# Two hybrid encoder layers on eight cores: a rewrite with subtiles, scheduled engines, packed weights and layer norm per subtile

## The chip, the cores and the metric

The kernel runs on the eight cores of one Trainium2 chip. Each core works alone on half of one sequence (2048 tokens, with 256 more in front as halo), in two passes of up to 1152 tokens. The metric is the device time of the slowest core in microseconds. The record sorts the executions into fast and slow ones. The first kernel's slow runs took 3552.8 and 3639.2 us, its fast ones 3271.4 and 3274.5. Only fast runs are compared. A ratio below is the record's: the fast runs of one kernel over the first kernel's fast runs of the same rounds. It is not quite the ratio of quoted medians. Short names: PE is the matmul engine (TensorE), PEld its weight loads, DVE is VectorE, ACT ScalarE, POOL GpSimd.

## The reference, cut to what matters

```python
for l in range(2):
    ada = (silu(c) @ w_ada[l] + b_ada[l])[:, None, :]          # conditioning, 6 x 1024 per sequence
    sh1, sc1, gt1, sh2, sc2, gt2 = split(ada, 6)
    h = x * (1 + sc1) + sh1
    z = h @ w_in[l] + b_in[l]                                  # 1024 -> 9216
    zb, zc, zx, zu, zv, zp, zg = split(z)
    y_a = (zb * conv3(zc * zx)) @ w_a_out[l]                   # branch A
    y_b = spatial_gating(gelu(zu), gelu(zv), ...) @ w_b_out[l] # branch B, norm of v, 128 x 128 blocks
    y_c = multiscale_pool(zp, w_pool[l], pool_scale[l])        # branch C
    g_a, g_b, g_c = split(sigmoid(zg), 3)
    x = layer_norm(ALPHA * x + gt1 * ((g_a*y_a + g_b*y_b + g_c*y_c) @ w_o[l]))
    h = x * (1 + sc2) + sh2
    up_a, up_g = split(h @ w_up[l] + b_up[l], 2)               # 1024 -> 2 x 2816
    f = gelu(conv3(up_a) + b) * up_g
    x = layer_norm(ALPHA * x + gt2 * (f @ w_down[l]))
```

## The kernel before

Data lie feature-major on chip: 128 features on the partitions, tokens along the free axis. One projection of all tokens of a pass fills three PSUM banks (PA or PB), and one VectorE or ScalarE instruction works on all of them.

```python
def fm_proj(lhs_list, rhs_fn, geo, P=None):
    off, nseg, seglen = geo                    # e.g. 3 pieces of 386 tokens
    if P is None:
        P = big_ps()                           # PA and PB in turn
    for j in range(nseg):
        for k in range(nk):
            mm(P[:, j, 0:seglen], lhs_list[k], rhs_fn(k, ...), k == 0, k == nk - 1, ...)
    return P[:, 0:nseg, 0:seglen]
```

Weights lie in memory as the reference has them; a load of 128 columns takes runs of 512 bytes. There are four slots of 4096 columns. All engines run in the order in which the program was written. The layer norm of a stage starts when the sums over all its tokens are there:

```python
def layer_norm_fm(c0, T, outs):                # T up to 1152
    ... S1, S2 = ones-matmuls over all tokens
    ts(mean, S1, 1.0 / D, ALU.mult)
    ... stt(rstd, S2, 1.0 / D, rstd, ALU.mult, ALU.subtract)
    act_op(rstd, rstd, AF.Sqrt, bias=epsc[:, 0:1])
    reciprocal(rstd)
    for c in range(8):
        tt(yh, r, meanf, ALU.subtract); tt(yh, yh, rstdf, ALU.mult)
        for dst_fn, sc_fn, b_fn in outs:       # back to xT, and the next h
            act_op(dst_fn(c), yh, AF.Identity, bias=b_fn(c), scale=sc_fn(c))
```

The input comes token-major and is transposed by TensorE (128 x 128 fp32), as is the output. The conditioning weights (24 loads of 1024 x 512) are worked off between other steps by a `tick()`.

## Time and profile before

| | |
|---|---|
| fast runs | 3271.4 and 3274.5 us |
| slow runs | 3552.8 and 3639.2 us |
| cores in the profiled run | 3261 to 3290 us, mean clock 0.913 to 0.922 |
| PE, DVE, ACT busy | 80, 47, 30% |

How to read it: PE is the busiest engine and the chain that ended last passes through it for 59% of the span, yet a fifth of the span it stands. The prediction shows the lines and cuts a layer into stages. Two more groups matter for what the change removes. They are from the view of instruction groups by shape; after the bar stand the busy time in us, the mean in ns, and the idle time of the engine just before with what ended it.

```profile
L324 ACT ACT_TABLE_LOAD x87 | 111.6, 1283 | 235.1 <-DVE tmp L328 86.8 <-DVE tmp L341 68.9 <-PE PA L304 35.2
...
L455 DVE RECIPROCAL tmp<-tmp 128x1152 f32<-128x1152 f32 x4 | 29.4, 7352 | 10.9 <-ACT tmp L324 10.9
```

A reciprocal of 1152 columns holds VectorE for 7.35 us while PE has nothing to do, and 87 activation table loads cost ScalarE 112 us.

### The profile page before, as it was taken

The numbers are of one execution on the slowest core, as the hardware profiler recorded it, in microseconds if no ns is written. First come the engines' busy times: TensorE is split into PE (matmuls) and PEld (weight loads), VectorE is DVE, ScalarE is ACT, GpSimd is POOL, SyncE is SP. The second block draws the span as 40 slices with busy tenths as digits, with TensorE's granted clock in tenths as the row PEclk, the third lists the DMA queues.
The fourth block names the chain that finished last, engine by engine and source line by source line (L and its number), as shares of the span: only waits on it lengthen the run. The fifth ranks groups of instructions, "written<-read, shape, count | busy, mean of one in ns | idle before, by whom it ended". The sixth has DMA issues, their size and how long they took to land.

```text
span 3290.1 us, 41682 instructions; the slowest of 8 cores (3261.2 to 3290.1 us)
## 1 busy us (share of the span) xinstructions
PE 2635.8 (80%) x17020; PEld 1594.4 (48%) x17020; DVE 1532.3 (47%) x1518; ACT 980.3 (30%) x905; POOL 285.0 (9%) x324
## 2 busy tenths in 40 slices
PE   3887798589598795888499699499959969949994
PEld 2553455356365563664355355255525535525552
DVE  3322435654643437454442433745364243374535
ACT  1112312443223313441222412444232241244412
POOL 1210000010110000101010000000101000001000
PEclk9998999799899997999699899799979989969997
DMA  9996736244564345447364232434536423234441
GB/s 172 122 131 93 109 58 92 39 65 54 56 77 66 52 71 64 53 65 83 122 70 72 39 54 50 64 52 56 63 29 77 65 39 58 39 51 58 52 53 58
DMA packets 348316, 225.39 MB, mean 69 GB/s; under 512 B 104416, under 2 KB 342112, under 8 KB 347616
## 3 DMA queue, kind: packets, MB, share of 16 engines
q0 software_dynamic: 341504, 198.20, 46.2%
q1 hardware_dynamic: 6624, 24.53, 2.2%
q8 instruction: 137, 2.24, 0.3%
q14 instruction: 51, 0.42, 0.0%
HBM read 412.50 MB, written 8.39 MB: 128 GB/s over the span
## 4 chain that ended last, share of the span: by engine, by line
PE 59%; DVE 18%; ACT 12%; DMA 5%; issue 4%; DVEq 0%; ACTq 0%; POOL 0%; SPq 0%; POOLq 0%
PE PA L304 31%; PE PB L304 23%; ACT tmp L324 7%; DVE tmp L341 5%; DVE tmp L328 3%; PE PC L304 2%; PE PD L304 2%; ACT L324 2%; DVE ubuf L328 2%; DMA wsl<-w_in 2%; DVE big L341 2%; DVE tmp L455 2%; DMA tmp<-xs 2%; ACT ubuf L324 1%; ACT hT L324 1%
## 5 line engine op out<-in xcount | busy, mean ns | idle before, releaser
L304 PE MATMUL PA<-hT,wsl 128*128 128x386 bf16 (+2 forms) x6336 | 1033.2, 320 | 295.4 <-DVE hT L345 217.2
L304 PEld LDWEIGHTS PA<-hT,wsl 128*128 128x128 bf16 x6336 | 618.5, 99 | 674.1 <-issue 333.0
L304 PE MATMUL PB<-hT,wsl 128*128 128x386 bf16 (+2 forms) x3264 | 521.8, 316 | 69.2 <-DVE big L341 49.7
L304 PEld LDWEIGHTS PB<-hT,wsl 128*128 128x128 bf16 x3264 | 312.6, 98 | 265.6 <-issue 97.4
L324 ACT ACTIVATE tmp<-PA,vecs_s 128x1158 f32<-128x1158 f32 (+2 forms) x200 | 229.8, 1149 | 685.7 <-PE PA L304 684.4
L341 DVE SCALAR_TENSOR_TENSOR tmp<-tmp,vecs_s 128x1156 f32<-128x1156 f32 (+2 forms) x240 | 318.1, 1325 | 238.4 <-ACT tmp L324 225.9
L324 ACT ACTIVATE tmp<-tmp,vecs_s 128x1158 f32<-128x1158 f32 (+2 forms) x208 | 246.1, 1183 | 420.3 <-DVE tmp L341 321.8
L304 PE MATMUL PB<-preT,wsl 128*128 128x386 bf16 (+2 forms) x1728 | 275.7, 313 | 4.1 <-DMA wsl<-w_a_out 3.5
L304 PE MATMUL PA<-big,wsl 128*128 128x384 bf16 (+2 forms) x1320 | 231.1, 333 | 8.3 <-DVE big L328 5.9
L277 POOL DMA_DIRECT2D wsl<-w_in x144 | 126.2, 886 | 1257.0 <-PE PA L304 548.3
L304 PE MATMUL PB<-big,wsl 128*128 128x384 bf16 (+2 forms) x1320 | 228.3, 331 | 0.0
L304 PEld LDWEIGHTS PB<-preT,wsl 128*128 128x128 bf16 x1728 | 166.6, 97 | 98.3 <-issue 5.5
L324 ACT ACTIVATE tmp<-xT 128x1152 f32<-128x1152 f32 (+2 forms) x72 | 77.4, 1085 | 387.4 <-DVE xT L341 387.4
L304 PE MATMUL PC<-wsl,hT 128*128 128x512 bf16 x560 | 142.6, 401 | 53.2 <-DVE tmp L328 48.9
L324 ACT ACT_TABLE_LOAD x87 | 111.6, 1283 | 235.1 <-DVE tmp L328 86.8
L304 PEld LDWEIGHTS PA<-big,wsl 128*128 128x128 bf16 x1320 | 130.5, 99 | 101.5 <-issue 11.1
L341 DVE SCALAR_TENSOR_TENSOR big<-PB,vecs_s,tmp 128x1158 bf16<-128x1158 f32 (+2 forms) x88 | 116.7, 1326 | 133.0 <-ACT tmp L324 114.6
L304 PEld LDWEIGHTS PB<-big,wsl 128*128 128x128 bf16 x1320 | 130.3, 99 | 90.0
L304 PE MATMUL PD<-wsl,hT 128*128 128x512 bf16 x560 | 143.8, 403 | 23.9 <-DVE tmp L328 16.0
L341 DVE SCALAR_TENSOR_TENSOR tmp<-PB,vecs_s,tmp 128x1158 f32<-128x1158 f32 (+2 forms) x48 | 63.6, 1326 | 186.5 <-PE PB L304 94.3
L277 POOL DMA_DIRECT2D wsl<-w_up x88 | 77.0, 883 | 690.3 <-PE PB L304 690.3
L328 DVE TENSOR_TENSOR big<-PB,tmp 128x1158 f32<-128x1158 f32 (+2 forms) x32 | 40.6, 1267 | 200.3 <-PE PB L304 160.7
(117 smaller groups left out, 1840.3 us busy)
## 6 DMA issues: line engine op xcount, KB each, us to landing
wsl<-w_in POOLq DMA_DIRECT2D x48, 1024.0 KB, 9.6
wsl<-w_up POOLq DMA_DIRECT2D x88, 512.0 KB, 7.8
wsl<-w_ada POOLq DMA_DIRECT2D x24, 1024.0 KB, 19.8
wsl<-w_in POOLq DMA_DIRECT2D x96, 256.0 KB, 6.2
wsl<-w_down POOLq DMA_DIRECT2D x32, 704.0 KB, 7.1
tmp<-xs SPq DMA_DIRECT2D x18, 512.0 KB, 4.7
wsl<-w_a_out POOLq DMA_DIRECT2D x8, 1024.0 KB, 8.2
wsl<-w_b_out POOLq DMA_DIRECT2D x8, 1024.0 KB, 12.1
```

The source lines that it names most:

```text
L277: items.append((lambda e, dst=dst, src=src: e.dma_start(out=dst, in_=src), (), (dst,)))
L304: R.op("pe", lambda e: e.matmul(o, l, r, start=start, stop=stop), reads=(l, r), writes=(o,), signal=signal)
L324: R.op("act", lambda e: e.activation(out=out, in_=in_, func=func, bias=bias, scale=scale), reads=rd, writes=(out,))
L328: R.op(eng, lambda e: e.tensor_tensor(out=out, in0=in0, in1=in1, op=op), reads=(in0, in1), writes=(out,))
L341: R.op(eng, lambda e: e.scalar_tensor_tensor(out=out, in0=in0, scalar=scalar, in1=in1, op0=op0, op1=op1), reads=rd, writes=(out,))
L455: R.op("dve", lambda e: e.reciprocal(out=rstd, in_=rstd), reads=(rstd,), writes=(rstd,))
```

## The change

The intent: PE should never stand. Nearly every instruction works on a subtile of at most 388 columns (512 in the v and z blocks), so that each projection takes one of eight PSUM banks, and a pass over the recorded program picks, engine by engine, what can start first. x and y are feature-major in memory, weights are packed so that each load reads one contiguous run per partition, the three gated branches are merged in one stage (with tanh in place of sigmoid, meant to spare table loads), and each subtile has its own layer norm, in which ScalarE's ln and exp take the place of the square root and the reciprocal. Cut to the core:

```diff
-class Rec:                       # engines in program order
+class Prog:
+    def schedule(self):          # list scheduling with a cost for each operation
+        while left:
+            for e in ENGS:
+                for op in avail[e]:
+                    est = op.ready if op.ready > f else f
+                    key = (est, op.prio)
+                    ...          # earliest start first, then program order
+            if op.dma:
+                t0 = max(est + cost + 1300.0, dma_free)
+                dma_free = t0 + op.nbytes / 320.0
...
-NSLOT = 4
-SLOT_ELEMS = 4096
+NW = 14                          # weight area: 14 units of 1024 columns
+UNIT = 1024
+class Units:                     # picks the free run of units that was given back longest ago
...
-        w_in = din("w_in", [DEPTH, D, DIN])
+        wmixa_d = din("wmixa", [DEPTH, 8, 128, 3 * UNIT])
+        wmrg_d = din("wmrg", [DEPTH, 8, 128, 5 * UNIT])
...
-        xs = din("xs", [TOK_IN, D])
+        xs = din("xs", [128, 8, TOK_IN])
...
+            wv = [wget(wv_d[l, hf], 4 * UNIT) for hf in range(2)]   # held through branch A
+            def mix_a(c):
+                h, w = wget(wmixa_d[l, c], 3 * UNIT)
+                for a, b in subs:          # 126..512, 512..896, 896..1152
+                    ...
+            for c in range(8):
+                mix_a(c)
+                tick()                     # one step of the conditioning, most with a load of 4 units
+                v_block(...)
...
+            for a, b in subs:
+                rs, rq = residual(l, 4, a, b, base, outs)
+                layer_norm(l, a, b, base, rs, rq, ...)
...
+                tt(st[:, 14:15], st[:, 13:14], cons[:, 1:2], ALU.pow, eng="pool")  # rsqrt of v blocks
```

## The prediction

Its 2453 us of PE work are 2409 us by the form N/2.4 + 2.5 ns and some 45 us for the conditioning matmuls, and this second term rested on a time for each that no trace shows. With it the sum came to 2743 us at full clock, and to 2800 us with the 57 us of step 7. That a tenth of the work is taken at 0.81 there is the author's guess, and so are the 20 us added to the first mixing in step 5. Rival (a) is the case that PE does half of its work at a clock of 0.81.

The form stands on the traces: without a wait between, 33 matmuls of 384 columns take 5.36 us in the first kernel (162.5 ns each, the form gives 162.5), bundles of 24 of 346 columns start 3.53 us apart there (146.9 ns, 146.7), and 16 of 512 columns take 3.46 us in the changed kernel (216 ns, 215.8). Of the dips of PEclk: from 2100 to 2120 us PE has no busy time and the clock is 0.50. The clock records of the first kernel hold 0.50, 0.81 and 1.00; on the core shown one of 0.81 lasts 15.1 us from 2072.8 us on, while PE works: 24 matmuls of 384 columns take 4.72 us there (197 ns each).

> **What bounds the kernel now.** I read the spans of the cores first: all eight lie between 3261 and 3290 us, so the profiled execution is an undisturbed one, like the 3274.5 us run. The other two runs (3552.8 and 3639.2 us) are 8.5 and 11% longer; I predict the undisturbed state. Then the page: the totals, the granted clock in 40 slices, the queue of weight loads, and the chain that ended last.
>
> ```profile
> PE 2635.8 (80%) x17020; PEld 1594.4 (48%) x17020; DVE 1532.3 (47%) x1518; ACT 980.3 (30%) x905; POOL 285.0 (9%) x324
> ...
> PEclk9998999799899997999699899799979989969997
> ...
> q0 software_dynamic: 341504, 198.20, 46.2%
> ...
> HBM read 412.50 MB, written 8.39 MB: 128 GB/s over the span
> ...
> PE 59%; DVE 18%; ACT 12%; DMA 5%; issue 4%; DVEq 0%; ACTq 0%; POOL 0%; SPq 0%; POOLq 0%
> ```
>
> No engine is full. The chain is 59% matmul; for the rest of the span the matmul engine waits for VectorE, ScalarE or a load. The dips of PEclk to 6 and 7 [...] stand where PE has stopped. To see where, I cut one layer of the second pass (1152 tokens) into stages: mixing up to the branch merge, output projection with layer norm, FFN up, FFN down, second layer norm.
>
> ```profile
> 1629.00:2050.00 421.00, 375.45 (x2260) 211.30 (x2261) 166.96 (x185) 113.20 (x109) 26.30 (x30) 0.97 0.37 56
> 2050.00:2142.00 92.00, 48.40 (x266) 26.78 (x265) 67.30 (x49) 37.30 (x30) 7.90 (x9) 0.75 0.44 57
> 2142.00:2323.00 181.00, 168.94 (x1013) 97.07 (x1011) 91.12 (x65) 79.89 (x64) 15.40 (x17) 0.99 0.41 53
> 2323.00:2410.00 87.00, 86.04 (x530) 51.44 (x527) 29.12 (x22) 10.46 (x9) 13.61 (x15) 1.00 0.63 70
> 2410.00:2455.00 45.00, 5.51 (x16) 2.02 (x17) 36.27 (x26) 24.38 (x19) 2.22 (x3) 0.53 0.18 17
> ```
>
> Columns: stretch, length, busy us of PE, weight loads, DVE, ACT, POOL, then clock, DMA share, GB/s. FFN down is at the floor: in the chain its bundles of 33 matmuls of 384 columns take 5.36 us, so 162.5 ns each. With N/2.4 + 2.5 ns per matmul [...] I worked out each stage's PE work from the shapes: 365 us for the first stage (56 lost), 31 for the second (61 lost), 170 for the third (11 lost), 86.5 for the fourth (0 lost), 1 for the fifth (44 lost). That is 172 us lost per layer and pass. Over the kernel I count 5.74 M columns in 15,980 projection matmuls, 2432 us, plus some 20 us for the 768 one-column matmuls of the conditioning. 3290 - 2452 leaves 838 us lost: 4 x 172 = 688, 65 us before the first mixing, some 80 of a slower first mixing (478 us for 1032 tokens, with 20 conditioning loads in it), the input transposes, and the last norm and store.
>
> [...] FFN down is dense on all cores for 87 us at clock 1.00, while 0.81 stands just in the output projection (2080 to 2100), where DVE is about 85% busy as well; the clock records have 24 to 61 us of it per core. [...] Here 198.2 MB in 341504 packets is 580 B each; 46.2% of 16 engines x 3290 us over the packets is 71 ns each, 8.2 B/ns, some 130 GB/s written in bf16 if all engines were full.
>
> **The change part by part.** (1) *PE work hardly moves.* From the new shapes: first pass 841.8k + 543.8k + 739.0k + 475.9k columns, second pass 2 x (926.8k + 611.6k), 5.68 M in some 17,000 matmuls: 5.68 M / 2.4 + 17k x 2.5 ns = 2409 us, [...] **2453 us**. What goes is one lead column block, input and output transposes (272 fp32 matmuls, about 67 us of busy time, on the path only at three points), and one of two full band products per block.
>
> (2) *Instruction sizes.* VectorE cost follows from two shapes of each kind:
>
> ```profile
> L341 DVE SCALAR_TENSOR_TENSOR tmp<-tmp,vecs_s 128x1156 f32<-128x1156 f32 x120 | 170.7, 1422 | 150.2 <-ACT tmp L324 144.0
> L341 DVE SCALAR_TENSOR_TENSOR tmp<-tmp,vecs_s 128x1036 f32<-128x1036 f32 x60 | 77.9, 1298 | 45.8 <-ACT tmp L324 42.6
> ...
> L328 DVE TENSOR_TENSOR tmp<-tmp 128x1152 f32<-128x1152 f32 x44 | 59.7, 1357 | 2.6 <-issue 0.3 <-ACT tmp L324 0.2
> ```
>
> (1422 - 1298)/120 = 1.03 ns a column, 228 ns fixed; with the 1032-column tensor op (1233 ns) the other kind is 1.04 and about 160. At 384 columns: 625 and 560 ns. Three pieces for one add two fixed costs, some 400 ns per operation, in return for a result that leaves a third as late. Sum for 384 tokens of mixing: branch A 8 x 4 x 625 = 20 us; v 12; u 10; merge 8 x (4 x 625 + 560) = 24.5; residual with sums 8 x (625 + 2 x 560) = 14; norm 17 x 560 = 9.5: 90 us against 131 us of PE. FFN: 22 x 3 x 625 = 41, plus 23.5: 65 against 86. Over 11.0 such subtiles about 1700 us of DVE (before 1532), 68 to 70% of the PE work: it rises, yet stays below. ScalarE (about 580 ns per 384-column activation, from 1227 ns at 1158 and 1127 at 1038) comes to some 100 us per subtile, 1100 in all. The 8 reciprocals (5.8 to 7.4 us each, about 54 us, all on the path) go, and so does the sqrt/sigmoid/gelu table switching (87 loads, 111.6 us, partly on the path) but for two loads around each norm.
>
> (3) *Norms per subtile.* The fifth stage (44 us lost) mostly vanishes: norms of the first two subtiles lie beside the down projection of the next (DVE 23.5 us against PE 29), and the last one's 15 to 20 us lie beside the next mixing's first subtiles, four bundles of 3.9 us. I leave 10 us lost. The second stage does less well: per subtile 10.5 us of PE against 23.5 us of residual and norm on DVE, so 31 against 70, and the FFN up that could fill it needs the norm's output, DVE and free banks. I put 30 us lost in place of 61.
>
> (4) *Mixing order.* v blocks between the branch A channels, z blocks between the u groups, eight single banks and twelve buffers instead of two large ones: I leave 15 us of 56. FFN up 5 of 11. Sum of the losses: 10 + 30 + 15 + 5 = 60 per layer and pass, **240 us**; if the overlaps work well, 160.
>
> (5) *Loads.* The bytes read stay (4 x 86 MB of weights, 50 of conditioning, 9 of x: about 410 MB); only the runs lengthen. Mid-kernel loads were hidden, so this is worth nothing there. At the start: four conditioning loads of 2.1 MB and x, 10 to 13 MB; between 20 and 60 us the trace moves 212 to 222 GB/s of x (f32) and conditioning weights (counted as bf16, so twice that read), from which I estimate 300 GB/s read with longer runs: about 45 us before mixing, in place of 65. In the first mixing 51 MB of weights and up to 20 conditioning loads, 93 MB in 357 us, 261 GB/s: [...] so I add 20 us. (6) *End.* No transposes; residual, norm and store of a 384-token piece, about 25 us.
>
> Sum: 2453 + 200 (between 160 and 240) + 45 + 20 + 25 = **2743 us** at full clock.
>
> (7) *Clock.* All of PE's work at 0.81 instead of 1.00 would cost 2409 x 0.23 = 555 us. [...] I take 10% of the work under it: 57 us. **2743 + 57 = 2800 us.**
>
> **Rivals.** (a) [...] the slow runs fit it (2432 x 1.23 plus the 650 us PE idles is 3640, the slowest run). Against it: full clock in dense FFN down and in FFN up at 50% DVE. With half of the work at 0.81 the time is near 3020. (b) *VectorE becomes the bound in long stages.* For it: 70% on average, over 100% in the output projection stage; small pieces pay the fixed cost three times. Against it: in mixing and FFN up DVE stays under 75% of PE. If the fixed order holds PE at 85%, 2850 to 2900. (c) *Everything overlaps*: losses of 25 us per layer and pass, [...]: 2453 + 100 + 90, about 2640. (d) *Loads bind*: if packed loads reach only 200 GB/s, the first mixing takes 465 us, 90 more.
>
> **Range and chances.** The centre is 2800; (c) gives the low end, a little below it 2620; (a) together with (b) the high end, 3040. Even with all work at 0.81 (2999 us plus some 200) the time would be about 3200, still 2% faster, so a slower result needs a fault that nothing in the profile suggests: faster 0.96, within 2% 0.03, slower 0.01.
>
> **What would show it.** PE busy above 90% of the span and DVE near 1700 us would confirm (2) to (4). The gap around the output projection should be the largest left; if PE is full there, I was too careful. No reciprocal and at most some 60 table loads. The DMA share should fall although GB/s rises. The prediction is wrong if the clock line shows 8 through most of the span, if DVE exceeds 85%, or if PE waits for weights outside the first mixing.

## The result, and the profile after

The changed kernel took 2856.8, 2860.9 and 2862.5 us in its fast runs and 3265.6 us in a slow one; the first kernel's fast runs were 3271.4 and 3274.5 us. The ratio is 0.8736 (95% interval 0.8719 to 0.8753): 413 us less. The totals of the new page, its slices, the queue of weight loads and the chain:

```profile
PE 2516.4 (88%) x16976; PEld 1573.8 (55%) x16976; DVE 1594.8 (56%) x3211; ACT 1089.6 (38%) x2030; POOL 248.5 (9%) x367
## 2 busy tenths in 40 slices
PE   0565978878999999989969999979999999989997
...
PEclk9886988999999999989989999989999999999999
DMA  9333665573334444643563434533323344353331
...
q0 software_dynamic: 107136, 197.97, 42.2%
...
PE 80%; DMA 14%; DVE 4%; ACT 2%; issue 1%; POOL 0%; ACTq 0%; SPq 0%; POOLq 0%; DVEq 0%
```

PE's share of the chain went from 59 to 80%, and the share of DVE and ACT together from 30 to 6. What is left over is DMA, which grew from 5 to 14%, and the slices say when: PE is at 0 to 8 tenths in eight of the first nine, whereas the second half is full but for a few. The queue moved the same bytes in a third of the packets.

Next the second pass (from 1490 us on) by stage, and below it the first 680 us of the same kernel. Columns as in the prediction: stretch, length, busy us of PE, PEld, DVE, ACT, POOL, clock, DMA share, GB/s. Stages: mixing up to the merge, output projection with norm, FFN; the same for the second layer; the end.

```profile
1490.00:1850.00 360.00, 357.66 (x2255) 208.27 (x2254) 187.48 (x338) 114.23 (x203) 37.56 (x56) 1.00 0.42 71
1850.00:1922.00 72.00, 52.12 (x273) 27.98 (x271) 60.18 (x122) 53.08 (x95) 4.22 (x6) 0.86 0.38 64
1922.00:2170.00 248.00, 247.13 (x1512) 146.76 (x1511) 160.80 (x297) 108.06 (x198) 15.24 (x21) 1.00 0.35 58
2170.00:2528.00 358.00, 356.55 (x2246) 207.34 (x2245) 186.21 (x337) 119.47 (x212) 37.32 (x57) 1.00 0.39 65
2528.00:2602.00 74.00, 54.19 (x281) 29.05 (x280) 63.52 (x129) 53.42 (x95) 3.52 (x5) 0.86 0.41 70
2602.00:2843.00 241.00, 241.00 (x1482) 144.05 (x1481) 152.43 (x281) 92.15 (x169) 12.94 (x18) 1.00 0.33 61
2843.00:2861.00 18.00, 1.02 (x5) 0.19 (x2) 9.78 (x20) 7.64 (x13) 0.00 (x0) 0.62 0.24 87
```

```profile
0.00:80.00 80.00, 5.30 (x133) 4.42 (x134) 6.28 (x30) 15.95 (x26) 8.75 (x17) 1.00 0.94 182
80.00:600.00 520.00, 384.16 (x2908) 236.49 (x2907) 185.08 (x385) 111.99 (x205) 47.23 (x69) 0.86 0.50 84
600.00:680.00 80.00, 58.03 (x370) 35.96 (x368) 68.25 (x154) 54.96 (x105) 10.07 (x15) 0.91 0.62 102
```

In the second pass PE stands some 20 us at each output projection, where DVE is 84 to 86% busy, and nowhere else but at the end; the 44 us after the FFN are gone. The first mixing is another matter: 520 us for work that the same shapes put at some 347 us (329 for the projections, 18 for conditioning). PE stands for 136 us of it, and for part of the rest it works at a lower clock (0.86 on average): the 72 matmuls of a channel take 12.3 to 13.5 us after a wait for conditioning and branch A, and 10.65 in the one channel that had no conditioning load before it. DMA engines are only half busy (share 0.50). The chain of that stretch, in order of time (start, length, what), shows one turn of a ring:

```profile
103.74 7.60 DMA mem<-wmixa
...
111.47 13.12 PE PS L453 x72
...
124.89 9.06 DMA mem<-wada
...
134.09 1.00 PE PS L453 x32
...
135.38 7.04 DMA mem<-wmixa
```

PE ends a channel, and only then is the conditioning load issued; it takes 9 us; PE uses it for 1 us, and only then is the next branch A load issued. No load runs ahead of its use. The program's own list of placements, printed while it was built, says why: in the first mixing the v blocks lie at units 4 to 7 and 8 to 11 of 14, each branch A block at 0 to 2 and each conditioning block at 0 to 3. Four plus three units do not fit into the six that are free, and the hole at 12 and 13 is too small even for a second branch A block. In the other three mixings the v blocks lie at 0 to 7 and branch A alternates between 8 and 11.

### The profile page after: what moved, and what is told of

The parts are those of the page before. It is cut to its first block, busy times and chain, and to the rows that moved or that the text cites. A ratio compares the mean times of both kernels' runs of the same rounds, so it can differ in the third digit from the quotient of the medians.

```text
span 2860.9 us, 42328 instructions; the slowest of 8 cores (2839.7 to 2860.9 us)
## 1 busy us (share of the span) xinstructions
PE 2516.4 (88%) x16976; PEld 1573.8 (55%) x16976; DVE 1594.8 (56%) x3211; ACT 1089.6 (38%) x2030; POOL 248.5 (9%) x367
## 3 DMA queue, kind: packets, MB, share of 16 engines
q0 software_dynamic: 107136, 197.97, 42.2%
## 4 chain that ended last, share of the span: by engine, by line
PE 80%; DMA 14%; DVE 4%; ACT 2%; issue 1%; POOL 0%; ACTq 0%; SPq 0%; POOLq 0%; DVEq 0%
PE PS L453 80%; DMA mem<-wada 5%; DMA mem<-wmixa 4%; DMA mem<-wmrg 3%; DVE xT L418 3%; DMA mem<-wp 1%; ACT hT L413 1%; DVE tmps L418 1%; ACT xT L413 1%; DMA xT<-xs 0%; DMA mem<-wo 0%; ACT mem L413 0%; ACT tmps L413 0%; DVE xT L434 0%; DVE tmps L434 0%
## 5 line engine op out<-in xcount | busy, mean ns | idle before, releaser
L453 PE MATMUL PS<-hT,mem 128*128 128x384 bf16 (+4 forms) x9600 | 1550.0, 319 | 176.5 <-DMA mem<-wmixa 81.7
L453 PEld LDWEIGHTS PS<-hT,mem 128*128 128x128 bf16 x9600 | 943.2, 99 | 724.3 <-issue 237.8
L453 PE MATMUL PS<-mem 128*128 128x384 bf16 (+3 forms) x4608 | 745.7, 316 | 29.1 <-DVE xT L434 18.7
L453 PEld LDWEIGHTS PS<-mem 128*128 128x128 bf16 x4608 | 452.1, 99 | 274.7 <-issue 40.2
L434 DVE SCALAR_TENSOR_TENSOR tmps<-PS,vecs_s,tmps 128x384 f32<-128x384 f32 (+4 forms) x624 | 358.8, 580 | 301.4 <-ACT tmps L413 171.8
L434 DVE SCALAR_TENSOR_TENSOR tmps<-tmps,PS 128x384 f32<-128x384 f32 (+3 forms) x288 | 150.0, 521 | 425.8 <-PE PS L453 228.8
L413 ACT ACTIVATE tmps<-PS,hgb 128x384 f32<-128x384 f32 (+3 forms) x288 | 160.3, 557 | 490.5 <-PE PS L453 490.5
L413 ACT ACTIVATE tmps<-PS,cfb,vecs_s 128x384 f32<-128x384 f32 (+1 forms) x264 | 168.5, 643 | 285.8 <-PE PS L453 284.8
L453 PE MATMUL PS<-mem,hT 128*128 128x512 bf16 x1120 | 256.7, 382 | 10.0 <-DMA mem<-wp 6.3
L434 DVE SCALAR_TENSOR_TENSOR mem<-PS,vecs_s,tmps 128x384 bf16<-128x384 f32 (+3 forms) x360 | 207.0, 578 | 30.4 <-ACT tmps L413 28.1
L418 DVE TENSOR_TENSOR xT<-xT,tmps 128x384 f32<-128x384 f32 (+3 forms) x384 | 173.5, 517 | 16.3 <-ACT tmps L413 15.8
L434 DVE SCALAR_TENSOR_TENSOR xT<-PS,der,xT 128x384 f32<-128x384 f32 (+3 forms) x192 | 109.1, 579 | 120.4 <-PE PS L453 119.9
L434 DVE SCALAR_TENSOR_TENSOR tmps<-tmps,vecs_s 128x384 f32<-128x384 f32 (+3 forms) x192 | 111.1, 583 | 50.0 <-ACT tmps L413 47.3
L434 DVE SCALAR_TENSOR_TENSOR tmps<-PS,vecs_s,bsb_s 128x384 f32<-128x384 f32 (+2 forms) x112 | 57.1, 529 | 110.0 <-PE PS L453 109.4
```

The source lines that it names most:

```text
L413: R.add("act", [lambda e: e.activation(out=out, in_=in_, func=func, bias=bias, scale=scale)], reads=[in_] + aps, writes=[out], cost=210 + ...
L418: R.add(eng, [lambda e: e.tensor_tensor(out=out, in0=in0, in1=in1, op=op)], reads=[in0, in1], writes=[out], cost=(165 + 1.042 * nfree(out) ...
L434: R.add("dve", [lambda e: e.scalar_tensor_tensor(out=out, in0=in0, scalar=scalar, in1=in1, op0=op0, op1=op1)], reads=rd, writes=[out], cos ...
L453: fns.append(lambda e, o=o, l=l, r=r, st=st, sp=sp: e.matmul(o, l, r, start=st, stop=sp))
```

## The experiments

My theory after this reading was **space**: the first mixing waits because a block can only be loaded once the block before it has been used up. The rival was **bandwidth** (rival (d) of the prediction): the first mixing reads some 40 MB of conditioning weights besides its own. Other runs ask where the gain came from.

### Conditioning loads in idle memory

```diff
         def ada_step(l, g):
-            h, w = wget(wada_d[l, g], 4 * UNIT)
+            if alt["on"]:                       # during branch A of the first mixing
+                o = F0 + (alt["n"] % 2) * 4 * UNIT      # the branch B buffer, idle until later
+                w = mem[:, o:o + 4 * UNIT]; dma("pool", w, wada_d[l, g], ...)
```

> Changed kernel with one thing moved: the eight conditioning weight loads that fall between the branch A channels of the first mixing land in memory that is idle at that time (the later branch B buffer), not in the weight area. Same bytes, same order of calls. Space theory: in the first 300 us the trace shows a ring (1 us conditioning matmuls, branch A load 7 us, 13 us of matmuls, conditioning load 9 us) with DMA engines only 0.3 busy, because a 4-unit conditioning block and a 3-unit branch A block do not fit together into the 6 units left; with the other space both loads run ahead, so eight times about 16 us vanish: 100 to 140 us less, 2860 to about 2740, ratio to the first kernel 0.83 to 0.845. Bandwidth theory: the same bytes in less time cannot come, so at most 30 us less, ratio 0.865 or above.

Measured: fast runs 2808.6 to 2810.5 us, ratio 0.8570 (0.8545 to 0.8595). That is 50 us less than the changed kernel: more than the 30 us that the bandwidth theory allows, half of what space promised. The promise was also counted too high: of the eight steps between the channels six are loads, by the program and by the trace, and six times 16 us are 96. The chain of the same stretch tells what was left:

```profile
149.59 7.24 DMA mem<-wmixa
...
157.23 12.80 PE PS L453 x72
...
170.32 8.59 DMA mem<-wmixa
```

The conditioning is off the chain, but branch A still loads one block at a time: the hole.

### And the v blocks placed low

```diff
-            wv = [wget(wv_d[l, hf], 4 * UNIT) for hf in range(2)]
+            wv = [wget(wv_d[l, hf], 4 * UNIT, at=hf * 4 * UNIT // QU) for hf in range(2)]
```

> The kernel of the first experiment (conditioning loads of the branch A channels in idle memory), and the two v weight blocks fixed at the low end of the weight area. In the first experiment each of the first eight channels still waited 7 us for its own branch A load: the v blocks had been put at units 4 to 11 of 14, which leaves a hole of four and one of two, and a block of three fits once. Low placement leaves six together. Place theory: eight times about 7 us less than the first experiment, 2810 to 2750 to 2765, ratio 0.838 to 0.845. If loads of the first mixing are bound by bandwidth: unchanged, 0.857.

Measured: median 2745.6 us, ratio 0.8377 (0.8364 to 0.8389), 116 us below the changed kernel. The chain of this run:

```profile
128.07 14.66 PE PS L453 x119
...
142.81 14.66 PE PS L453 x119
...
157.54 14.66 PE PS L453 x119
```

Channel follows channel with nothing between, and 14.66 us is what the shapes give: 72 branch A matmuls, 24,720 columns by the form N/2.4 + 2.5 ns, which the traces bear out (see above the prediction), 10.5 us; 16 of 512 columns, 3.45 us; and 0.7 us is left for the 32 conditioning matmuls. From 80 to 300 us the DMA share is 0.72 (108 GB/s), where the changed kernel has 0.33 (54 GB/s): the loads were not at their limit there. Of the 116 us, 96 are won by the end of branch A: in the chains of the two kernels the load after it lands at 311.4 and at 215.0 us.

### The placement alone

The same edit of the v blocks, without moving the conditioning loads.

> The changed kernel with only the v blocks fixed at the low end of the weight area; the conditioning loads stay in that area. Six units are then together, but a conditioning block (4) and a branch A block (3) still need seven, so between channels with a conditioning step the ring stays: space theory says at most 20 us less, 2840 to 2865, ratio 0.867 to 0.875. If the hole alone was the cause and the conditioning loads are innocent: 2760 or below, ratio under 0.845.

Measured: fast runs from 2820.4 us, ratio 0.8610 (0.8585 to 0.8635): 40 us less, twice what I allowed. The ring still stands where a conditioning load falls between two channels (8 to 11 us for it, then 7 to 8 us for branch A), but the one pair of channels with none between now runs on, and the waits for merge weights before 600 us fall from 32.5 to 16.0 us, since later blocks fall into place differently: replaying the program's own choice of places puts all eight merge blocks of three units at 10 to 12 in the changed kernel, and at 6, 8, 9 or 11 here. Alone the two edits give 50 and 40 us; together they give 116.

### The same pressure where no conditioning loads are

```diff
+            hold = None if first else units.get(UNIT // QU, 0, NW * UNIT // QU, UNIT // QU)
             for c in range(8):
                 mix_a(c)
...
+            if hold is not None:
+                units.put(hold, UNIT // QU)
```

> Changed kernel with one unit of the weight area withheld during branch A of the two mixings of the second pass, so two branch A blocks (3 units each) no longer fit side by side. No byte is added and there are no conditioning loads in this pass. Space theory: each of 16 channels now waits for its own load, 7 us less what the v block between (3.5 us of matmuls) hides: 60 to 110 us more, ratio 0.89 to 0.91. Bandwidth theory: no change, ratio 0.873 within 0.5%.

Measured: 2946 us and up, ratio 0.8993 (0.8955 to 0.9032): about 90 us more, 5.6 us for each of the 16 channels. PE's wait for branch A loads, in the list of waits of the changed kernel and then of this run (us in total, times, longest):

```profile
PE PS L453 <- DMA mem<-wmixa: 81.7, 10, 20.9
...
PE PS L453 <- DMA mem<-wmixa: 137.2, 23, 20.4
```

That is 55 us more; with them the mean clock of the cores fell from 0.953 to 0.944, and from 1490 us on PE is busy for 1341 us in place of 1310, which is most of the rest. No byte was added. So lack of space makes such a wait by itself, and with the two runs above I take the space theory as shown for branch A of the first mixing.

### Norms in time, not in size

```diff
             for a, b in subs:
-                rs, rq = residual(...); layer_norm(...)
+                rr.append((a, b, residual(...)))
+            alln = [sums of all subtiles]    # those of the third lie in an idle v buffer
+            for a, b, (rs, rq) in rr:
+                layer_norm(..., after=alln)      # its first matmul also waits for alln
```

> Changed kernel, with the sums of all subtiles of a stage awaited before the first norm of that stage (the norm is per subtile in size but no longer in time). If the norm beside the next projection is a main source of the gain, the eight stage ends cost about 25 to 35 us more each: 200 to 280 us, ratio 0.93 to 0.96. Rival: VectorE is full at those ends anyway, so the norms just move: under 80 us more, ratio below 0.90.

Measured: 2952 us and up, ratio 0.9013 (0.8987 to 0.9039): 95 us more, 12 us for each of the eight stage ends. Both expectations missed, the rival's by little. PE's longest wait is now for h, which each stage needs first (the changed kernel's line, then this run's):

```profile
PE PS L453 <- ACT hT L413: 12.5, 3, 10.0
...
PE PS L453 <- ACT hT L413: 144.3, 18, 31.7
```

The rival is right in part: the waits at the residual (xT and tmps of L434, 61.8 us in the changed kernel) fall to 5.4 us, so some of the loss only moved. VectorE is not full there, as it assumed, but 84 to 86% busy at the output projections of the second pass. Letting a norm lie beside the projections that follow is worth some 95 us net, about a quarter of the gain.

### Program order

```diff
                 for op in avail[e]:
+                    if op.idx != nextup[e][-1]:      # the next of this engine as written
+                        continue
```

> Changed kernel, every engine executing in program order in place of the list-scheduled order. If the scheduled order is what lets a norm of one subtile lie beside the projection of the next, the matmul engine now waits in each of the 24 norms for the residual sums and in the mixing for each eviction just ahead of it: 150 to 300 us more, ratio 0.92 to 0.97. Rival, that small subtiles with eight banks do it alone and the order is of little account: under 50 us more, ratio below 0.89.

Measured: 3492 us, ratio 1.0656 (1.0631 to 1.0682). The rewrite without its scheduled order is slower than the first kernel, and twice as much is lost as I had expected at most. The waits of PE in this run:

```profile
PE PS L457 <- DMA mem<-wmixa: 356.5, 29, 29.9
PE PS L457 <- DVE lnb L422: 177.3, 34, 29.6
PE PS L457 <- DMA mem<-wada: 107.6, 14, 16.3
PE PS L457 <- DMA mem<-wu: 79.7, 4, 23.9
```

The first line surprised me. The weight loads are issued by POOL, which also computes the rsqrt of the v blocks. The waits of POOL from 1760 to 2100 us, where no conditioning is loaded:

```profile
POOL stat L422 <- DVE stat L430: 270.1, 9, 76.3
POOL mem L449 <- PE PS L457: 45.0, 3, 19.0
```

POOL stood 270 of 340 us before an operation on one column, waiting for the statistics of a block whose matmuls come after the present channel; the next load stood behind it. The control lets POOL alone go by the schedule:

> Matmul, vector and scalar engines in program order, the queue that issues the weight loads in scheduled order. Program order everywhere cost 630 us, of which the matmul engine waited some 600 for weights and 177 for norm sums. If the scheduled order pays through the load queue (in program order an rsqrt step of the v blocks stands between the loads on that queue): 2950 to 3080 us, ratio 0.90 to 0.94. If it pays through the order of the matmuls: above 3300, ratio above 1.0.

Measured: fast runs from 3122 us, ratio 0.9536 (0.9517 to 0.9555). The wait for branch A loads falls from 356.5 to 35.3 us, the wait for norm sums stays (8.0 us in the changed kernel):

```profile
PE PS L457 <- DVE lnb L422: 177.2, 35, 33.1
...
PE PS L457 <- DMA mem<-wmixa: 35.3, 6, 20.4
```

So of the 630 us some 365 are the order of loads on their queue and some 265 the order on PE, DVE and ACT, most of that the norms (169 us more wait for their sums). The result lies between the two numbers, nearer to the first.

### Parts done alone in the first kernel

Packed weights in the first kernel (each `wload` takes one contiguous row per partition, nothing else):

> The first kernel with packed weights alone: every weight load reads contiguous rows per partition, nothing else changes. By the prediction packing is worth nothing in the middle of the kernel and something at the start and in the first mixing, where loads were waited for: 30 to 90 us less, ratio 0.973 to 0.99. Rival: small packets slow the loads everywhere, ratio below 0.96.

Measured: 3258 us and up, ratio 0.9940 (0.9920 to 0.9960): about 20 us, less than the low end. The queue of weight loads took 37.3% of the engines in place of 46.2, but PE had hardly waited for it: from 65 to 543 us, 45 us for weight loads in the first kernel and 25 us in this run, which is the gain.

```profile
q0 software_dynamic: 105280, 198.19, 37.3%
```

The packed rows, 1882 B on the average, took 185 ns each (37.3% of 16 engines over 3260 us), so each engine wrote 10.2 B/ns while it was busy; the first kernel's 580 B took 71 ns, 8.2 B/ns.

Feature-major x and y in the first kernel:

```diff
-                for half, P in enumerate((PC, PD)): ... 8 transposes a block, scaled copies out of PSUM
+            for c in range(8):
+                xc = xT[:, c, 0:t1 - t0]
+                dma("sp", xc, xs[:, c, t0:t1], ...); ts(xc, xc, ALPHA, ALU.mult)
```

> The first kernel with feature-major x and y alone: eight loads of one feature block each straight into place, scaled there, no transposes in or out, eight stores. Part theory: 20 to 30 us less in the middle where x of the second pass is loaded and transposed, 10 to 20 at the end, little at the start (conditioning loads set that): 30 to 60 us less, ratio 0.982 to 0.991. Rival: the transposes were hidden beside the loads, ratio above 0.995.

Measured: 3227 us, ratio 0.9841 (0.9819 to 0.9863): 52 us, in the range given. The two parts, added up and not run together, are near 70 of the 413 us.

### A kernel faster than both

```diff
+                o = F0 + (alt["n"] % 2) * 2 * NPRE + (alt["n"] // 2 % 2) * 4 * UNIT   # four idle places
...
             for j in range(8):
                 merge(j)
-                tick()
...
+        load_x(*xp[0], 0)                    # first subtile; the others wait for the conditioning
```

> Meant to beat both kernels: all conditioning loads up to the end of branch A of the first mixing go to four idle places of the later branch buffers, none falls in the branch merge (they go on in the FFN, where there is room), the first x subtile is loaded before the others, which wait for the conditioning. The v blocks then come to lie low by themselves. Space theory: start 80 to about 50 us, no waits in branch A, about 40 us less in the merge: 2660 to 2720 us, ratio 0.81 to 0.83. Bandwidth theory: not under 2790.

Measured: fast runs from 2732 us, ratio 0.8343 (0.8329 to 0.8357): faster than both, but just above the range. PE still waited 56 us for conditioning loads, which I put down to those beside the u groups, and 31 us for the first branch A block, which stood behind the v blocks. Both were then addressed: no `tick()` beside the u groups, and the first branch A block loaded ahead (with the v blocks placed low and some small constant loads moved behind them).

> The previous best, with two remaining waits addressed. There the matmul engine still waited 56 us for conditioning loads (six of them 8 to 18 us each beside the u groups, where one place serves them all) and 31 us for the first branch A block, which was queued behind the v blocks. Here no conditioning load falls beside the u groups (the rest go to the FFN) and the first branch A block is loaded ahead of the v blocks. Space and queue theory: 45 us less at the u groups and about 20 at the start, 2733 to 2660 to 2680, ratio 0.812 to 0.82. If the loads are bound by bandwidth they will be waited for in the FFN instead: about 2730.

Measured: 2710.8 to 2718.5 us, ratio 0.8280 (0.8262 to 0.8298), the fastest of all, and again some 40 us short. Two reasons show. First, the 56 us had been misread: the list covered 0 to 700 us, and 40.6 us of it lie before 80 us, at the start. From 80 to 700 us the run before had only this:

```profile
PE PS L453 <- DMA mem<-wada: 15.3, 4, 13.7
```

That fell to 1.8 us, and the waits of PE for conditioning and branch A at the start fell only from 71.8 to 65.2 us; together that is the 19 us gained. Second, at the start the bandwidth rival is right. The first stretches of this run:

```profile
0.00:40.00 40.00, 2.98 (x96) 2.81 (x96) 4.42 (x23) 1.49 (x2) 10.72 (x19) 1.00 0.97 186
40.00:80.00 40.00, 9.33 (x64) 4.67 (x64) 5.57 (x12) 17.01 (x27) 0.74 (x1) 0.83 1.06 193
80.00:120.00 40.00, 33.06 (x241) 19.77 (x242) 18.63 (x41) 9.53 (x18) 4.17 (x6) 0.83 1.01 157
```

For the first 120 us the DMA engines are full (share 0.97 to 1.06), and whatever is put first makes something else late. So at the start loads bind by their rate, as far as the DMA share shows it; in the mixing after it they were bound by space.

## Why the prediction was right or wrong

The predicted 2800 us lies 2% below the measured 2861, inside the range, and faster by over 2% came true. The mechanism was right: DVE and ACT left PE's way. The first pass was put 174 us too low, the second pass 56 and the clock 57 us too high. These errors partly cancel, so that the total came within 2% is in part luck. The sum without the clock, 2743 us, was 1427 for the second pass (1302 of work, 100 lost, 25 at the end) and 1316 for the first; measured are 1371 and 1490.

- **Step 1, PE work 2453 us.** Confirmed where PE is full: the 14.66 us channels, and FFN stages of 241 to 248 us with PE 100% busy. The conditioning matmuls were put too high at 45 us; the profile has 23 us busy (the 20 us for the first kernel were nearer).
- **Step 2, instruction sizes.** The median of the residual step is 608 ns where I had 625; DVE 1595 us where I had 1700. DVE stayed 56% busy, ACT at 1090 us. Table loads fell from 87 to 17.
- **Steps 3 and 4, losses in the second pass.** Too high. The output projection costs 20 us and not 30, mixing 2 and not 15, the FFN with its norm 1 and not 15. The second pass came out 56 us shorter than its share of the sum. I had named the output projection as the largest gap left. In the second pass it is; in the whole kernel the first mixing is, with 136 us.
- **Step 5, loads, is the step that failed.** It gave 45 us to the start and 20 to the first mixing, from bytes and rate. The start took 80 us. The first mixing lost 173 us where steps 4 and 5 together had 35. Of its cause, the runs show 116 us to be places in the weight area (96 us in branch A, the rest after it), in place of the rate that I had reckoned with. I had read in the diff that the area has 14 units and that branch A holds two v blocks of 4 beside its own 3 and the conditioning's 4, and had not added them up: 8 + 3 + 4 is 15. What is left of the first mixing in the placement run (merge weights, conditioning beside the u groups) was only shortened, not taken apart.
- **Step 7, the clock.** 57 us were put on a tenth of PE's work at 0.81. In the profiled fast run no core has a record of 0.81 (the first kernel has 24 to 61 us of it per core), not even at the output projections where DVE is 84 to 86% busy, so the term is 0. Rival (a) fell for the fast state. The slow run of 3265.6 us has the cores of one die at a mean of 0.812 to 0.813 and those of the other at 0.952 to 0.954. What sets the clock to 0.81 is not shown by any run here. I had put all work at 0.81 at some 3200 us, "still 2% faster". That sum left out terms of its own: 2743 + 555 are some 3300 us, no gain, and the slow run agrees with that. The reading that 0.81 stood just in the output projections of the first kernel was not quite so either: cores 2 and 3 also have 4.9 us of it at 1790 us and 5.1 us at 2606 us.
- **Rivals.** (b) VectorE as the bound holds only at the output projections. (c) is close to the kernel with the waits mended, 2715 us against 2640. (d) is right for the start alone.
- **The signs.** Held: no reciprocal, 17 table loads, the share of the weight queue down from 46.2 to 42.2% while the mean rate rose from 69 to 78 GB/s, no 0.81 in the clock, DVE under 85%. Not held: PE is at 88% and not above 90, and PE waited for weights outside the first mixing, 75 us at the start and 16 us after 600 us.

The cause of the gain, in the order of what the runs show: scheduled order, on the load queue as on the other engines (in program order all the rest is 6.6% slower than the first kernel; with the load queue alone scheduled it is 4.6% faster); norms beside the projections that follow, some 95 us; transposes, some 50; packing, some 20. These do not add up to 413, since each was undone or done by itself. The size of the subtiles, the merging of the branches and the change of table functions were not undone, so what they are worth is not shown.

## What to carry to other kernels

Add up, stage by stage, the sizes of all blocks that must be in a weight area at the same time, the held ones, the present one and the one being loaded; if the sum exceeds the area by one unit, or the free part has a hole, loads can no longer run ahead: in branch A of the first mixing PE then waited on the chain for each conditioning load (9.06 us in the turn shown) and each branch A load (7.04 us), while the DMA share looked harmlessly low (0.33). An engine that issues loads should compute nothing that waits for other engines, unless a schedule keeps the loads ahead of it (without one, POOL stood 270 of 340 us here and PE waited 356.5 us for branch A loads). Subtiles and a scheduled order belong together: in program order the rewrite lost here, and more than half of that loss was the order on the load queue.
